# Two-layer S5, Hyena and pooling step: layer 1's scan values computed in the opening, filters and root spread behind the modulation, sums of squares on TensorE, convolutions in turn with gates

## The chip, the core and the metric

One core of a Trainium2 chip runs the whole program. TensorE (PE) multiplies, VectorE (DVE) and ScalarE (ACT) do elementwise work, GpSimd (POOL) does a part of it too, and SyncE (SP) issues most transfers. The metric is the device time of one execution in microseconds (us), lower is better; times are compared as medians of runs.

## The reference

Two layers work on 128 context tokens and 512 latent tokens (T = 640 columns), model width 1024. Cut to what the change touches:

```python
def trunk_layer(x, mod, h0_re, h0_im, p, l):
    shift, scale, gate = jnp.split(mod[:, None, :], 3, axis=-1)      # mod = silu(cond) @ w_mod + b_mod
    h = rms_norm(x, p['norm_g'][l]) * (1.0 + scale) + shift
    proj = h @ p['w_in'][l]
    u_a, g_a, u_b, g_b, u_c, g_c, m = jnp.split(proj, IN_SPLIT_POINTS, axis=-1)
    y_a, st_re, st_im = s5_branch(u_a, ...)       # 32 groups, 64 complex states, two directions
    y_b = hyena_branch(u_b, ...)                  # short convolution, then gated long convolutions
    y_c = pool_branch(u_c, ...)
    ...                                           # silu gates, three branch projections, w_out
    return x + gate * out, st_re, st_im
```

`s5_discretise` turns each state's parameters into a step factor a and an input matrix `bb` = k * b (complex). `hyena_filters` makes a layer's long filters from positions and weights alone; a bias times the input is added to each long convolution. Neither depends on x.

## The kernel before

**Layout.** Channels lie on the partitions, the 640 tokens on the free axis, as two halves of HT = 320 columns or as context (LS = 128 columns) and latents. Every matrix product is a split one: a float32 operand becomes a rounded high part and the rest, and three matmuls are summed: `mm` with (hhi, wh), (hlo, wh), (hhi, wl), lines 261 to 263. A window of 128 output channels is 48 mm of 320 columns. Weights come by SP in pieces `wr`; ACT makes `wh`, DVE `wl` (lines 238, 239). All engines run their instructions in the order in which a scheduler has put them; a DMA stands in its engine's queue, and an instruction behind one that waits has to wait too.

**Opening.** `s5_load`, `setup`, `mlp` (hidden layer of the Hyena filters, for both layers), `load_x0` (x and the position embedding). `square` (line 582) squares each of eight 128-channel blocks on ACT and adds them up on DVE into `acc` (line 589); `rsum` sums over partitions by tiny matmuls `ssq` (line 599). `s5_disc` computes both layers' factors and powers in small DVE operations. `mod_chunk` multiplies the conditioning with w_mod, four chunks of four loads `wm` (line 401) and matmuls `modp`; `mod_turn` transposes the result (`modt`). `s5_disc2` finishes layer 0's scan values: the product `bb` (`cmul`, lines 693 to 698), `phases` (lines 846 to 851), and powers copied by ACT into `pi` and `po`; layer 1's powers and factors go to DRAM (`pwd`, `rsd`). `rinv` makes 1/sqrt of the mean square by three Newton rounds, spreads it over the partitions (`rdg` on DVE, `rbc` on PE, copy `rr` on ACT), and `make_h` forms h for each half: `ht`, `hhi`, `hlo` (lines 656 to 665). `filter` makes a quarter of a layer's Hyena filters: `fw` and `fwp` (line 511) on PE, `hx` and `hq` on DVE, the bias row `br` added by two one-partition DVE operations (lines 522, 523), then `fps` matmuls and a store `hd`.

**A layer.** `u_a` computes four windows and stores them to `ud`; `load_u` reads them back as `ug` in S5 layout. Then eight S5 blocks of four groups: `s5_gen` makes matrices `i`, transposes them on PE (`trp`), forms the local kernel (`khp`), stores it to `kd` and reads it back by eight loads as `mt`, and makes phases `tt`; `s5_run` multiplies (`pz`), scans on DVE, and multiplies back (`yp`). After each block two or three items of a list `beside` run: twelve convolution windows (`conv_u`: ACT copies `raw`, DVE adds the two neighbours in `vx`), then four gates (`gate_b`), then four windows computed ahead (`ahead`). The list goes from front to back:

```python
beside = [lambda i=i: self.conv_u(l, i, vx[i // 4][:, i % 4, :], SP) for i in range(12)]
beside += [lambda i=i: self.gate_b(l, i, S, vx[2]) for i in range(4)]
beside += [lambda i=i: self.ahead(l, 40 + i, AF.Tanh, 0.5, SP) for i in range(4)]
```

**Boundary.** While layer 0's output projection runs, two of layer 1's four filter quarters are made; then `rinv` on POOL, `make_h`, the other two quarters. `s5_prep` loads layer 1's powers and factors and computes there what `s5_disc2` computed for layer 0, with the complex product on POOL.

## Time and profile before

| | |
|---|---|
| median of 3 runs | 1528.35 us (1527.81 to 1533.11) |
| profiled execution, its own time | 1534.17 us |
| its span from first to last instruction | 1532.4 us |
| PE, DVE, ACT, POOL busy | 1435.3, 1125.5, 672.0, 524.9 us |
| mean granted TensorE clock | 0.976 |

Busy time is the sum over the span; the stretches below show where an engine idles. The clock is the share of full speed that the throttle granted.

### The profile page before, as it was taken

How to read it: one execution, taken by the hardware profiler on the slowest of the kernel's cores; microseconds unless marked ns; L12 is line 12 of the kernel's file. 1: busy time of each engine (PE TensorE's matmuls, PEld its weight loads, DVE VectorE, ACT ScalarE, POOL GpSimd, SP SyncE). 2: the span in 40 equal slices, each digit the busy share in tenths (PEclk: the TensorE clock that was granted, in tenths of full speed). 3: DMA queues.
4: the chain of work that ended last, by engine and by line, in shares of the span. 5: the costliest groups of instructions: out<-in, count | busy, mean ns of one | idle time of the engine just before them, and what ended most of it. 6: DMA issues, size and time to landing. Idle time of an engine off the chain costs nothing.

```text
span 1532.4 us, 28365 instructions
## 1 busy us (share of the span) xinstructions
PE 1435.3 (94%) x10812; PEld 1372.2 (90%) x10812; DVE 1125.5 (73%) x1951; ACT 672.0 (44%) x1454; POOL 524.9 (34%) x473
## 2 busy tenths in 40 slices
PE   3998899999999999999998897989999999999997
PEld 1688888999999998999997787989999999999996
DVE  8996998854777795555678879896557778866665
ACT  3574545434333342344345644544443334344443
POOL 0033433500343334553323733443003444166401
PEclk9899999999999999999998899999999999999998
DMA  9535122244322246444752342223622223322154
GB/s 313 188 112 132 57 72 70 71 146 123 99 71 77 76 134 234 157 151 139 230 159 81 110 113 68 71 71 94 172 89 81 83 70 106 115 83 83 35 178 153
DMA packets 120464, 178.74 MB, mean 117 GB/s; under 512 B 33944, under 2 KB 58152, under 8 KB 119817
## 3 DMA queue, kind: packets, MB, share of 16 engines
q1 hardware_dynamic: 115737, 170.58, 36.5%
q0 software_dynamic: 1152, 5.77, 1.1%
q8 instruction: 85, 1.39, 0.4%
q10 hardware_dynamic: 3440, 0.59, 0.2%
q14 instruction: 50, 0.41, 0.1%
HBM read 152.71 MB, written 24.18 MB: 115 GB/s over the span
## 4 chain that ended last, share of the span: by engine, by line
PE 68%; DVE 15%; DMA 6%; issue 5%; ACT 3%; SPq 2%; POOL 1%; POOLq 0%; ACTq 0%; DVEq 0%
PE mm L261 15%; PE mm L263 15%; PE mm L262 15%; PE mm L333 3%; PE mm L335 3%; PE mm L334 3%; DVE wl L239 2%; PE inva L1145 1%; SPq L914 1%; DVE i L874 1%; PE invb L1145 1%; PE yp L976 1%; PE modp L404 1%; DVE vx L1003 1%; DVE hlo L665 1%
## 5 line engine op out<-in xcount | busy, mean ns | idle before, releaser
L261 PE MATMUL mm<-hhi,wh 128*128 128x320 f32 x1408 | 446.1, 318 | 15.3 <-ACT raw L996 9.0
L263 PE MATMUL mm<-hhi,wl 128*128 128x320 f32 x1408 | 440.4, 314 | 8.5 <-DVE wl L239 6.3
L262 PE MATMUL mm<-hlo,wh 128*128 128x320 f32 x1408 | 442.4, 314 | 0.5 <-DVE hlo L659 0.4
L239 DVE TENSOR_TENSOR wl<-wr,wh 128x512 fp32r<-128x512 f32 x316 | 265.9, 843 | 114.4 <-ACT wh L238 111.5
L238 ACT CAST wh<-wr 128x512 fp32r<-128x512 f32 x316 | 195.5, 619 | 269.1 <-PE mm L262 188.9
L261 PEld LDWEIGHTS mm<-hhi,wh 128*128 128x128 f32 x1408 | 269.9, 192 | 20.8 <-ACT raw L996 10.0
L263 PEld LDWEIGHTS mm<-hhi,wl 128*128 128x128 f32 x1408 | 269.5, 192 | 9.5 <-DVE wl L239 6.8
L262 PEld LDWEIGHTS mm<-hlo,wh 128*128 128x128 f32 x1408 | 270.1, 192 | 1.7 <-DVE hlo L659 1.2
L262 PE MATMUL mm<-mlo,wh 128*128 128x320 f32 x256 | 79.6, 312 | 0.5 <-DVE mlo L242 0.4
L261 PE MATMUL mm<-mhi,wh 128*128 128x320 f32 x256 | 79.1, 312 | 0.5 <-ACT wh L238 0.4
L263 PE MATMUL mm<-mhi,wl 128*128 128x320 f32 x256 | 78.8, 309 | 0.4 <-DVE wl L239 0.4
L873 POOL TENSOR_TENSOR ow<-cw,po 128x512 f32<-128x512 f32 x32 | 41.9, 1328 | 96.6 <-PE yp L976 96.5
L875 POOL TENSOR_TENSOR i<-i,i 128x1024 f32<-128x1024 f32 x16 | 40.5, 2529 | 100.6 <-DVE i L873 71.8
L1244 DVE SCALAR_TENSOR_TENSOR mth<-mth,mm 128x320 f32<-128x320 f32 x64 | 31.1, 486 | 52.5 <-PE mm L263 52.5
L1246 POOL TENSOR_TENSOR macc<-macc,mth 128x320 f32<-128x320 f32 x32 | 35.0, 1099 | 86.4 <-DVE mth L1244 86.4
L239 DVE TENSOR_TENSOR wl<-ws,wh 128x512 fp32r<-128x512 f32 x48 | 42.7, 889 | 29.7 <-ACT wh L238 28.6
L333 PE MATMUL mm<-hhi,wh 128*128 128x320 f32 x192 | 59.9, 312 | 0.0
L335 PE MATMUL mm<-hhi,wl 128*128 128x320 f32 x192 | 59.4, 309 | 0.0
L334 PE MATMUL mm<-hlo,wh 128*128 128x320 f32 x192 | 59.4, 309 | 0.0
L238 ACT CAST wh<-ws 128x512 fp32r<-128x512 f32 x48 | 29.8, 621 | 60.2 <-PE mm L334 32.3
L1052 POOL TENSOR_TENSOR ps<-pu 128x663 f32<-128x663 f32 x8 | 12.3, 1540 | 120.4 <-ACT pu L1045 120.4
L1246 POOL TENSOR_TENSOR acc<-acc,mth 128x320 f32<-128x320 f32 x32 | 37.7, 1179 | 44.4 <-DVE mth L1244 44.3
(421 smaller groups left out, 3809.9 us busy)
## 6 DMA issues: line engine op xcount, KB each, us to landing
wr<-w_in SPq DMA_DIRECT2D x224, 256.0 KB, 2.6
wm<-w_mod SPq DMA_DIRECT2D x48, 512.0 KB, 5.4
wr<-w_out SPq DMA_DIRECT2D x48, 256.0 KB, 3.0
hd<-hs SPq DMA_DIRECT2D x32, 256.0 KB, 2.3
hsr<-hd SPq DMA_DIRECT2D x32, 256.0 KB, 2.6
mt<-kd SPq DMA_DIRECT2D x128, 32.0 KB, 1.8
wr<-w_br_a SPq DMA_DIRECT2D x16, 256.0 KB, 2.6
wr<-w_br_b SPq DMA_DIRECT2D x16, 256.0 KB, 2.7
```

The source lines that it names most:

```text
L238: nc.scalar.copy(hi, src)
L239: nc.vector.tensor_tensor(out=lo, in0=src, in1=hi.bitcast(F32), op=ALU.subtract)
L261: nc.tensor.matmul(ps[i], wh[:, ks], at(hi, k, sl), start=(k == 0), stop=False)
L262: nc.tensor.matmul(ps[i], wh[:, ks], at(lo, k, sl), start=False, stop=False)
L263: nc.tensor.matmul(ps[i], wl[:, ks], at(hi, k, sl), start=False, stop=(k == kt - 1))
L333: nc.tensor.matmul(out, wh[:, ks], xh, start=(k == 0), stop=False)
L334: nc.tensor.matmul(out, wh[:, ks], xl, start=False, stop=False)
L335: nc.tensor.matmul(out, wl[:, ks], xh, start=False, stop=(k == 3))
L873: eng.tensor_tensor(out=out[:, r], in0=hb(r), in1=pb(0), op=ALU.mult)
L875: e.tensor_tensor(out=out, in0=out, in1=tmp, op=ALU.add)
L1244: v.scalar_tensor_tensor(out=o[:, sl], in0=th[:, sl], scalar=1.0, in1=ps, op0=ALU.add, op1=ALU.mult)
L1246: nc.gpsimd.tensor_tensor(out=acc[:, sl], in0=acc[:, sl], in1=th[:, sl], op=ALU.add)
```

## The change

1. The opening computes the scan values of both layers (`s5_disc2` loops over the layers). Layer 1's five tiles go by POOL's queue to DRAM (`vd`), and `s5_prep` only loads them. `s5b`, the loaded matrix, and `phq` now share one buffer (tag s5b, one copy). Memsets of `bp` and `bf` move to POOL.
2. In the opening each square is summed directly on PE (`square_pe`); the Newton rounds come before the modulation, the spread (`rspread`) behind its last transpose; filter work on PE also behind that transpose, and w3 and the windows behind the last wm load.
3. At the boundary `rinv` runs on DVE, and `make_h` takes segments of columns (context and latents in the opening).
4. The bias row is added on PE by one more matmul per case, with one row of contraction.
5. `beside` mixes convolutions with ahead windows and gates, two light items to three heavy ones, the last four convolutions first.

```diff
@@ filter
-                                 stop=(i == len(ws) - 1))
+                                 stop=(i == len(ws) - 1 and t not in (2, 4)))
+            if t in (2, 4):
+                r = slice(0, 1) if t == 2 else slice(64, 65)
+                nc.tensor.matmul(fp if t == 4 else fw[:, t], self.k(C_BR)[r], br[r], start=False, stop=True)
...
-        v.tensor_tensor(out=hx[0:1, 2], in0=hx[0:1, 2], in1=br[0:1], op=ALU.add)
-        v.tensor_tensor(out=hq[64:65], in0=hq[64:65], in1=br[64:65], op=ALU.add)
@@ new
+    def square_pe(self, X, kk, half, ps):
...
+        nc.scalar.activation(sq, X[:, kk, half * HT:half * HT + HT], AF.Square)
+        for j in range(nh):
+            c = half * nh + j
+            nc.tensor.matmul(ps[:, c:c + 1], sq[:, j * 64:j * 64 + 64], self.k(C_ONE)[:, 0:1],
...
@@ scan values
-        self.cmul(nc.gpsimd if l else nc.vector, Q, self.bb[:, 0], self.bb[:, 1], kb(kre), kb(kim), sm[:, 0], sm[:, 1], [G, H], "cb")
+        sm = Q.tile([P, 2, G, H], F32, tag="s5b", name="s5b", bufs=1)
         nc.sync.dma_start(sm, self.I['s5m'][l, :, 0:2])
...
+        self.cmul(nc.vector, Q, bb[:, 0], bb[:, 1], kb(kre), kb(kim), sm[:, 0], sm[:, 1], [G, H], "cb")
...
     def s5_disc2(self, Q, S, pw, rs):
         nc = self.nc
-        nc.scalar.dma_start(self.pwd, pw[:, :, :, 1])
-        nc.scalar.dma_start(self.rsd, rs[:, :, 1])
-        self.s5_bb(Q, S, 0, rs[:, 6, 0], rs[:, 7, 0])
-        self.s5_vals(S, 0, pw[:, :, :, 0], rs[:, :, 0])
...
+        for l in range(DEPTH):
+            tl = self.s5_tiles(S if l == 0 else Q)
+            self.s5_vals(Q, l, pw[:, :, :, l], rs[:, :, l], *tl)
+            if l:
+                for d, t in zip(self.vd, tl):
+                    nc.gpsimd.dma_start(d, t)
...
     def s5_prep(self, S):
...
+        tl = self.s5_tiles(S)
+        for d, t in zip(self.vd, tl):
+            self.nc.sync.dma_start(t, d)
+        self.s5_open(S, 1, tl)
@@ opening
-                    dd = self.s5_disc(Q, SP)
+                    ssq = self.PS.tile([P, 512], F32, tag="mm", name="ssq", bufs=3)[0:64, 0:2 * (HT // 64)]
                     for kk in range(KD):
-                        self.square(X, kk, 0)
+                        self.square_pe(X, kk, 0, ssq)
...
+                    y = self.rinv((0, 1), nc.vector, "mm", ps=ssq, spread=False)
+                    self.s5_disc2(Q, SP, *self.s5_disc(Q, SP))
+                    for n in (2, 3, 0, 1):
+                        self.mod_turn(0, n, self.mod_chunk(0, n, M, "mm"), "mm")
+                    with tc.issue_after(self.last_mt.ins):
+                        rr = self.rspread((0, 1), y, "mm")
...
+                    with tc.issue_after(self.last_wm.ins):
+                        self.filter_load(0, F, wins, fr, fh)
...
+                self.make_h(0, X, ((0, LS, 0), (LS, T, 1)), rr)
+                with tc.issue_after(self.last_mt.ins):
+                    for o in range(2):
+                        for hf in range(2):
+                            self.filter(0, o, hf, F)
@@ boundary
-                            rr = [r for r, _ in self.rinv((0, 1), nc.gpsimd, "mm")]
-                            for half in range(2):
-                                self.make_h(l + 1, X, half, rr[half])
+                            rr = self.rinv((0, 1), nc.vector, "mm")
+                            self.make_h(l + 1, X, ((0, HT, 0),), rr)
+                            self.make_h(l + 1, X, ((HT, LS, 0), (LS, T, 1)), rr[:, HT:])
@@ layer
+            heavy = [lambda i=i: self.conv_u(l, i, vx[i // 4][:, i % 4, :], SP) for i in (*range(8, 12), *range(8))]
+            gates = [lambda i=i: self.gate_b(l, i, S, vx[2]) for i in range(4)]
+            ahead = [lambda i=i: self.ahead(l, 40 + i, AF.Tanh, 0.5, SP) for i in range(4)]
+            light = ahead[:2] + gates + ahead[2:]
+            beside = []
+            for i in range(4):
+                h, g = heavy[3 * i:3 * i + 3], light[2 * i:2 * i + 2]
+                beside += [h[0], g[0], h[1], h[2], g[1]]
```

SP's queue in the opening, before (`w_349` is w3, `s5m` holds the S5 matrices, `hyb` the bias rows):

```order
L474 DMA w_349<-hyp 64x1024
L476 DMA wins<-win 128x512 x5
L401 DMA wm<-w_mod 128x1024 x4
L794 DMA s5b<-s5m 128x1024
L811 DMA cw<-s5m 128x1024
L496 DMA br<-hyb 1x256 x4
L252 DMA wr<-w_in 128x512 x3
L401 DMA wm<-w_mod 128x1024 x4
```

The same queue in the changed kernel, from the fifth wm load on (`w_626` is w3):

```order
L403 DMA wm<-w_mod 128x1024 x2
L254 DMA wr<-w_in 128x512 x2
L403 DMA wm<-w_mod 128x1024 x2
L254 DMA wr<-w_in 128x512
L403 DMA wm<-w_mod 128x1024 x3
L815 DMA s5b<-s5m 128x1024
L403 DMA wm<-w_mod 128x1024 x5
L476 DMA w_626<-hyp 64x1024
L478 DMA wins<-win 128x512 x5
```

The filter's loads went from ahead of the first wm to behind the last, and layer 1's `s5b` load now stands ahead of five of the sixteen wm loads.

DVE's queue at the start of layer 1, before, from the second `wl` split of u_a on:

```order
L239 TENSOR_TENSOR wl<-wr,wh 128x512
L846 TENSOR_TENSOR phq<-cst,rsl 128x608
L848 TENSOR_TENSOR ph<-cst,rsl 128x608
L847 TENSOR_SCALAR phq<-phq 128x608
L239 TENSOR_TENSOR wl<-wr,wh 128x512
L849 TENSOR_TENSOR ph<-ph,phq 128x608
L239 TENSOR_TENSOR wl<-wr,wh 128x512
L850 TENSOR_TENSOR phq<-cst,rsl 128x608
L851 TENSOR_TENSOR ph<-ph,phq 128x608
L672 MEMSET ua_9719 128x8
L239 TENSOR_TENSOR wl<-wr,wh 128x512
L873 TENSOR_TENSOR i_9993<-bb,pi 128x512
```

The same place in the changed kernel:

```order
L241 TENSOR_TENSOR wl<-wr,wh 128x512 x2
L943 TENSOR_TENSOR tt<-ph 128x352 x2
L897 TENSOR_TENSOR i_10003<-bb,pi 128x512
L898 TENSOR_TENSOR i_10004<-bb,pi 128x512
L241 TENSOR_TENSOR wl<-wr,wh 128x512
```

The six phase operations are gone, and the first block's `tt` and `i` stand right behind the first splits.

ACT's queue in layer 0's fourth S5 block, before (`z` copies take the starting states, `kh` is the local kernel):

```order
L906 COPY kh<-khp 128x240
L892 COPY bf_453<-bb 128x8x16
L238 CAST wh<-wr 128x512
L956 COPY z<-rsl 64x8
L957 COPY z<-rsl 64x8
L996 COPY raw<-mm 128x320
L925 ACTIVATE d_2676<-cst,rsl 128x82 x4
```

The block in the changed kernel that answers to it:

```order
L930 COPY kh<-khp 128x240
L916 COPY bf_504<-bb 128x8x16
L1006 ACTIVATE gu<-gu 128x324
L240 CAST wh<-wr 128x512
L1020 COPY raw<-mm 128x320
L980 COPY z<-rsl 64x8
L981 COPY z<-rsl 64x8
```

The convolution's first `raw` copy moved from behind the z copies to ahead of them here; in four of layer 0's eight blocks it stands behind them in the changed kernel.

## Rows read from the trace of the kernel before

**Rows 1.** The page's busy times: us, share of the span, instructions.

```profile
PE 1435.3 (94%) x10812; PEld 1372.2 (90%) x10812; DVE 1125.5 (73%) x1951; ACT 672.0 (44%) x1454; POOL 524.9 (34%) x473
```

**Rows 2.** Table of stretches: length, busy us (instructions), PEclk, DMA share, GB/s.

```profile
0.00:60.00 60.00, 32.17 (x154) 15.95 (x155) 51.87 (x174) 25.82 (x55) 1.47 (x6) 0.91 0.93 305
100.00:345.00 245.00, 224.43 (x2025) 218.11 (x2024) 197.69 (x263) 116.13 (x293) 92.28 (x61) 0.97 0.34 95
345.00:800.00 455.00, 453.85 (x3178) 434.79 (x3176) 297.90 (x538) 178.17 (x344) 158.06 (x161) 1.00 0.43 137
800.00:900.00 100.00, 83.99 (x589) 78.01 (x590) 78.88 (x132) 57.69 (x131) 45.88 (x43) 0.90 0.39 112
900.00:1050.00 150.00, 134.10 (x1295) 130.14 (x1294) 135.44 (x186) 75.14 (x195) 66.48 (x40) 0.97 0.24 69
1100.00:1500.00 400.00, 397.47 (x2769) 392.96 (x2770) 283.17 (x497) 167.17 (x325) 144.12 (x141) 1.00 0.32 96
```

**Rows 3.** PE's waits, whole span: waiting line, releaser, us, times, longest.

```profile
PE yp L974 <- DMA mt<-kd: 19.5, 9, 3.7
...
PE mm L261 <- ACT raw L996: 9.0, 4, 3.1
PE mm L263 <- DVE wl L239: 6.7, 3, 5.0
PE pz L944 <- DMA ug<-ud: 5.0, 2, 3.3
PE modp L404 <- DMA wm<-w_mod: 4.3, 1, 4.3
```

**Rows 4.** PE's timeline at the boundary: start, duration, line, tile; idle before.

```profile
799.08 0.28 PE L599 MATMUL ssq<-cst,acc 128*64 128x1 f32 x2
...
808.24 0.39 PE L599 MATMUL ssq<-cst,sq 128*64 128x1 f32 x4
...
820.09 1.85 PE L635 MATMUL rbc<-rdg,cst 64*128 64x320 f32 x4
...
824.96 0.31 PE L261 MATMUL mm<-hhi,wh 128*128 128x320 f32 x1
...
894.85 0.28 PE L944 MATMUL pz<-ug,it 128*64 128x82 f32 x1 [1.69 <-DMA ug<-ud]
```

**Rows 5.** The mm alone, by stretches: PE, PEld, DVE, ACT busy, PEclk.

```profile
71.20:145.00 73.80, 44.92 (x286) 42.09 (x286) 0.00 (x0) 7.15 (x16) 1.00 0.42 112
824.90:894.80 69.90, 51.77 (x292) 48.13 (x292) 0.00 (x0) 7.10 (x16) 0.90 0.43 120
```

**Rows 6.** Prices: timeline rows; the last is fps alone in a stretch.

```profile
854.73 1.65 DVE L850 TENSOR_TENSOR phq<-cst,rsl 128x608 f32<-128x608 f32 x1
...
855.69 1.85 POOL L697 TENSOR_TENSOR bb<-cb,cb 128x512 f32<-128x512 f32 x1
...
44.09 0.69 DVE L695 TENSOR_TENSOR cb<-rs,s5b 128x512 f32<-128x512 f32 x1
...
22.68 0.48 DVE L589 TENSOR_TENSOR acc<-acc,sq 128x320 f32<-128x320 f32 x1
...
39.61 1.99 PE L511 MATMUL fw<-w,fh 64*128 64x256 f32 x8
...
71.20:145.00 73.80, 15.13 (x115) 14.07 (x114) 6.58 (x12) 1.00 0.42 112
```

**Rows 7.** DMA: a POOL-queue load's row, and the tile wm's issues and landings.

```profile
fr<-fdft POOLq DMA_DIRECT2D x2, 1152.0 KB, 6.3
...
L401 SPq DMA_DIRECT2D wm<-w_mod x16: 327/328/384, 15.2 to 51.5; - x16
...
DMA to landing us min/median/max: 4.1/4.7/5.4
```

**Rows 8.** ACT's timeline in layer 0's fourth S5 block.

```profile
197.59 0.20 ACT L956 COPY z<-rsl 64x8 f32<-64x8 f32 x1 [6.89 <-DVE z L955]
```

**Rows 9.** Layer 0: first `ht` on DVE, first `pz` on PE.

```profile
71.23 0.53 DVE L661 SCALAR_TENSOR_TENSOR ht<-X,sg,rr 128x320 f32<-128x320 f32 x1
...
144.99 0.28 PE L944 MATMUL pz<-ug,it 128*64 128x82 f32 x1 [3.32 <-DMA ug<-ud]
```

More of the change, by code (lines that the diff above doesn't have):

```diff
@@ L116, in constants @@
     cst[:, CO[C_MAG]] = MAGIC
+    for r in (0, 64):
+        cst[r, CO[C_BR] + r] = 1.0 / (1.0 + f32(0.05))
     fmax = 15
@@ L608, in newton, with rinv @@
         e.tensor_tensor(out=y, in0=y, in1=t, op=ALU.mult)
-    def rinv(self, halves, e, tag="b", root=False):
+    def rinv(self, halves, e, tag="b", root=False, ps=None, spread=True):
         nc = self.nc
@@ L613, in rinv @@
         n = nh * len(halves)
-        ps = self.rsum(halves, tag)
+        if ps is None:
+            ps = self.rsum(halves, tag)
         x = self.N.tile([64, n], F32, tag="rx", name="rx", bufs=2)
@@ L643, in new_h, with make_h @@
         self.hlo = self.HP.tile([P, KD, T], F32R, tag="hlo", name="hlo")
-    def make_h(self, l, X, half, rr):
+    def make_h(self, l, X, segs, rr):
         nc = self.nc
         sm, sg = self.smod[l]
-        t0 = half * HT
+        base = segs[0][0]
         for kk in range(KD):
-            t = self.N.tile([P, HT], F32, tag="ht", name="ht", bufs=2)
-            for s, e, _, ci in self.segs(half):
+            t = self.N.tile([P, segs[-1][1] - base], F32, tag="ht", name="ht", bufs=2)
+            for s, e, ci in segs:
@@ L668, in u_a @@
+                nc.scalar.activation(hi, tv, AF.Identity, bias=b)
+                nc.vector.scalar_tensor_tensor(out=lo, in0=tv, scalar=b, in1=hi.bitcast(F32),
+                                               op0=ALU.add, op1=ALU.subtract)
     def u_a(self, l, S, uas):
@@ new lines, in s5_disc2, with s5_vals @@
+        self.s5_open(S, 0, keep)
+    def s5_vals(self, Q, l, pw, rs, bb, ph, pi, po, rsl):
+        nc = self.nc
+        self.s5_bb(Q, bb, l, rs[:, 6], rs[:, 7])
+        gv = lambda a: a.rearrange("p t g -> p g t")
+        for r, ri, ro in ((0, 0, 0), (1, 2, 1)):
+            nc.scalar.copy(pi[0:64, ri], gv(pw[0:64, r, 0:8, :])[:, :, ::-1])
+            nc.scalar.copy(pi[64:P, ri], gv(pw[64:P, r, 0:8, :]))
+            nc.scalar.copy(po[0:64, ro], gv(pw[0:64, r, 1:9, :]))
+            nc.scalar.copy(po[64:P, ro], gv(pw[64:P, r, 1:9, :])[:, :, ::-1])
+        nc.scalar.mul(pi[:, 1], pi[:, 2], -1.0)
+        nc.scalar.mul(po[:, 2], po[:, 1], -1.0)
+        nc.scalar.copy(rsl, rs[:, 0:6])
+        v = nc.vector
+        sh = [P, G, NA + NBW]
+        mb = self.k(C_MT).unsqueeze(1).to_broadcast(sh)
+        fb = lambda i: rs[:, 1 + i].unsqueeze(2).to_broadcast(sh)
+        q = Q.tile([P, 2, G, H], F32, tag="s5b", name="phq", bufs=1).rearrange("p r g h -> p (r g h)")
+        q = q[:, 0:G * (NA + NBW)].rearrange("p (g m) -> p g m", g=G)
+        v.tensor_tensor(out=q, in0=mb, in1=fb(0), op=ALU.mult)
+        v.tensor_scalar(q, q, MAGIC, MAGIC, op0=ALU.add, op1=ALU.subtract)
+        v.tensor_tensor(out=ph, in0=mb, in1=fb(1), op=ALU.mult)
+        v.tensor_tensor(out=ph, in0=ph, in1=q, op=ALU.subtract)
+        v.tensor_tensor(out=q, in0=mb, in1=fb(2), op=ALU.mult)
+        v.tensor_tensor(out=ph, in0=ph, in1=q, op=ALU.add)
@@ L1406, in layer @@
             self.load_u(l, S)
-            beside = [lambda i=i: self.conv_u(l, i, vx[i // 4][:, i % 4, :], SP) for i in range(12)]
-            beside += [lambda i=i: self.gate_b(l, i, S, vx[2]) for i in range(4)]
-            beside += [lambda i=i: self.ahead(l, 40 + i, AF.Tanh, 0.5, SP) for i in range(4)]
+            heavy = [lambda i=i: self.conv_u(l, i, vx[i // 4][:, i % 4, :], SP) for i in (*range(8, 12), *range(8))]
[6 more added lines that the diff above has]
+                beside += [h[0], g[0], h[1], h[2], g[1]]
             for b in range(NB):
```

127 lines of the change are left out of this document (47 added, 80 removed).

## The prediction

> **What bounds the kernel now.** I read the page's busy times first. TensorE (PE) is busy for 94% of the span of 1532.4 us [rows 1], so some 97 us of idle PE are all that can be won, and what a change is worth depends on where that idle time lies. The table of stretches shows it [rows 2]. Three stretches matter: 0 to 60 us, PE busy 32.17 of 60; 100 to 345 us (the end of layer 0's u_a and its S5 blocks), idle 20.6; and 800 to 1050 us (the boundary to layer 1, then its S5 blocks), idle 16.0 + 15.9. The granted clock is 0.97, 0.90 and 0.97 in the last three of these. From 345 to 800 and from 1100 to 1500 us PE is full (453.85 of 455, 397.47 of 400) at clock 1.00; no edit takes PE work from there, and I carry them over unchanged. In the S5 stretch from 900 us DVE is as full as PE (135.44 of 150).
>
> The list of PE's waits [rows 3] says who ends the idle time: the S5 blocks' `mt` loads 19.5 us in 9 waits, the `raw` copies of the convolutions 9.0 in 4, `wl` 6.7 in 3, `wm` 4.3 in one.
>
> Last I followed the boundary in PE's timeline [rows 4]. The sums of the root start at 799.08, their last group at 808.24, the spread of the root (`rbc`) only at 820.09, the first mm of u_a at 824.96, the first S5 block's `pz` at 894.85: 95.8 us in all. What an mm costs is read from the stretches of mm alone [rows 5]: 286 in 44.92 us at clock 1.00 before layer 0's pz, 0.157 each, but 292 in 51.77 us at 0.90 before layer 1's.
>
> **Layer-1 boundary.** *Ceiling.* From 800 to 900 us PE idles 16.0 us, and a clock of 0.90 over 100 us is 10 us of lost work: 26 us. *Removed.* Six phase operations on DVE (the longest kinds 1.65 [rows 6]), six products on POOL (up to 1.85 [rows 6], while the same product took 0.69 on DVE in the opening [rows 6]) and eleven ACT copies. In the trace they ran around 855 us [rows 6] beside u_a, with the `wl` splits queued among them on DVE, and the S5 transposes behind them. *Moved.* The root's Newton steps go from POOL to DVE, a few us earlier; all filter operations now stand ahead of rbc or before the boundary, and 192 mm of u_a stand in one run behind. *Added.* Five loads of the stored values, 1.72 MB, where two small loads stood. They wait for make_h's last read of X, whose memory they take. The nearest row is POOL's `fr`, 1152 KB landing in 6.3 us [rows 7]: the S5 preparation can wait 0 to 6 us for them; I take 2, since u_a runs meanwhile and the first that is needed is the smallest case (DVE's `tt`).
>
> The chain after, on PE, from the first root sum: root, spread and first mm at about 22 instead of 25.9. Then 286 mm (45), small S5 matmuls (2), gaps as in layer 0 (2 to 5): pz at 71 to 74, against 95.8, so 22 to 25 us. PE work that moved ahead of the boundary comes off: 30 filter matmuls at 0.13 (115 in 15.13 us [rows 6]) and four bias matmuls at 0.5 (below), 6 us. Less the 2 us for the loads, **15 us** gained. Bounds: 6 (the loads cost 6 and the root gets no earlier) and 20 (the loads cost nothing).
>
> **S5 blocks of both layers.** Convolutions and gates now take turns; a gate or ahead window needs no pass on DVE over 642 columns, so the early blocks, which held three and two convolutions, ask less of DVE. At 197.59 us two `z` copies on ACT ran after 6.89 us of waiting for DVE [rows 8], and a raw copy that PE needed stood right behind them. In that block the raw copy now stands ahead of the z copies, but in four of layer 0's eight blocks it still stands behind; there it is DVE's shorter queue that must help. So of the 9.0 us of raw waits I expect two thirds to go, 6 us, and with them a part of the work lost to low clock: 0.97 over 245 and 150 us is 12 us, of which I take 2. The mt waits stay in the sum: their chain (kernel matmuls, copy, store to `kd`, eight loads) is unchanged. **8 us** for two layers. Bounds: 0 (gate waits take the raw waits' place) and 22 (all of raw, half of mt and a third of the clock's loss).
>
> **Opening.** DVE loses 14 `acc` additions of 0.48 [rows 6], 6.7 us, and gains layer 1's product and phases, twelve operations of about 0.7, 8.4 us. ACT gains eleven copies. The squares' sums are 80 tiny matmuls, 40 more, where PE idles: nothing; if that cover is gone, some 3 us. The memsets and stores that POOL takes over hold up nothing on POOL itself, which has no other work there. The filters' DVE work that ran ahead of make_h moves behind it.
>
> There the change has a hitch. Layer 1's matrix load `s5b` shares one buffer with layer 0's, so it waits until DVE is through with layer 0's phases, which I put at 45 us from DVE's rows; five of the 16 `wm` loads stand behind it on SP's queue. The last wm was issued at 51.5 us, and they land in 4.1 to 5.4 us [rows 7]; I now put the last landing at 55 to 61, and the last modulation transposes at 58 to 64, so the first `ht` comes at 60 to 67 instead of 71.23 [rows 9]. But all of the filters' PE work now stands behind the modulation, where a good part of it ran between the wm loads before. From there to pz: 16 `fw` and four `fwp` at 0.5 (four took 1.99 us [rows 6]), 10 us; 168 filter matmuls, 22; 292 mm, 46; small ones 3; eight bias matmuls.
>
> A bias matmul has one row of contraction and 256 f32 columns. None like it is in the trace; the nearest row is the opening's f32 fw, 0.5 us, and I take that; between 0.13 (the filters' f32r ones) and 0.5 it is 1 to 4 us for layer 0. Sum 85 us, with 3 for gaps: pz at 146 to 152 against 144.99 [rows 9]. **4 us** lost, bounds −5 (the bias matmuls and gaps cheap, wm early) and +12.
>
> On such a matmul the Trainium skill ("TensorE: Matmul & The Clock Gate") says that a matmul's time goes by its columns and not by its contraction rows. By that the bias matmul costs as much as fw, which is the value taken; no row here shows it.
>
> **Sum.** 4 − 15 − 8 = −19 us. Against the profiled execution's 1534.2 that is 1515; it was 5.8 us over the median of the three runs, 1528.35. Taken off the median: **1509**. A measurement of this kernel tells about 0.5%, 7.6 us, from no change.
>
> **Rivals.** *A: the turn in the S5 blocks brings nothing* (0.22). DVE is what the blocks wait for; the raw waits become gate waits and mt stays. For it: 19.5 us of mt against 9.0 of raw, DVE at 90%. Against: a raw copy stood idle behind a DVE wait. Time 1528 − 15 + 4 = 1517. *B: everything comes in* (0.18). The opening gains 5, the boundary 20, S5 18: 1485. It needs the s5b wait to end by 40 us. *C: no change* (0.1). The boundary gives 8 because the loads or DVE hold it, S5 nothing, the opening takes 4: 1524. *D: slower* (0.1). One mechanism, the queue behind `s5b` on SP. ACT has 16 copies of layer values ahead of the copy that empties the third modulation chunk, and if DVE's phases end at 65 us instead of 45, wm lands 20 us later, the first ht comes at 82 to 87, and pz at 168 to 174. With 23 us of gain left, the change turns slower when layer 0's pz comes after 168; at 35 us of loss in the opening the time is 1540.
>
> A rule that bears on D: by the Trainium skill ("SBUF — State Buffer", on DVE and DMA issued by GpSimd) GpSimd writes such a transfer's descriptors over a port that DVE can hold, and it advises the queue of ACT or SP. The stores of layer 1's values move to GpSimd's queue while DVE is at its fullest (51.87 of 60 [rows 2]). No row here has such a store beside a busy DVE: `fr` went out at the start. If it holds, memory that the new h takes over comes free late, as in D, without any late wm.
>
> **Numbers.** The forecast's own case has 0.4 (1501 to 1516). The range that leaves out about 0.2 goes from B's end to a little past C's: **1484 to 1528**. Faster by over 0.5% (under 1520.7): 0.4 + 0.18 (B) + 0.16 of A's 0.22, 0.74. Within 0.5%: C and the rest of A, 0.16. Slower: 0.10.
>
> **What would show it.** Boundary: the first mm 22 us after the first root sum, no scan-value operations on DVE or POOL there, pz at 71 to 75. S5: raw waits of 3 us in all at most, mt still 15 to 20, the clock 0.98 or more. Opening: first ht at 60 to 67, layer 0's pz at 146 to 152, a wm wait in PE's list. I am wrong if layer 0's pz comes after 160, if waits for gates or `tt` replace the raw waits, or if layer 1's pz waits over 6 us for the five loads.

## The result: slower, and the profile after

The changed kernel took 1541.88 us (median of 4, 1540.41 to 1544.38) against 1528.08 for the kernel before, measured beside it; the ratio is 1.0085 (1.0059 to 1.0111). That is slower by more than the 0.5% bound, and outside the range 1484 to 1528. The two profiled executions lie 6.2 us apart (span 1532.4 and 1538.6), since that of before was high among its runs (1534.17) and that of after its lowest (1540.41): the traces below account for 6.2 of the 13.8 us, the rest shows in medians only. Of all executions behind the ratios of this document one is left out, of the kernel e18 below: it took 6443.72 us. (The section on the kernel calls LS the context's 128 columns; LS is the 512 latents.)

First the page of the kernel after, busy times over the span:

```profile
PE 1460.0 (95%) x10964; PEld 1383.4 (90%) x10964; DVE 1089.2 (71%) x1920; ACT 671.9 (44%) x1445; POOL 516.5 (34%) x465
```

Against [rows 1] PE is busy 24.7 us longer, with 152 records more, while the span grew by 6.2: PE's idle time fell by 18.5 us, and more than that came back as work. To see where, both spans are cut at the same landmarks (first `pz` of layer 0, its last `trp`, first root sum, first `pz` of layer 1, its last `trp`). The kernel before, then the kernel after; columns: stretch, length, busy of PE, PEld, DVE, ACT, POOL, granted clock, DMA share, GB/s:

```profile
0.00:145.00 145.00, 108.23 (x700) 85.71 (x700) 121.36 (x301) 75.19 (x168) 29.75 (x28) 0.94 0.61 189
145.00:321.70 176.70, 163.37 (x1499) 158.61 (x1500) 152.74 (x205) 84.14 (x215) 69.33 (x42) 0.95 0.26 75
321.70:799.10 477.40, 476.25 (x3400) 457.05 (x3398) 309.58 (x555) 185.43 (x362) 159.37 (x166) 1.00 0.44 138
799.10:894.90 95.80, 79.79 (x541) 73.75 (x540) 76.62 (x128) 55.92 (x128) 45.88 (x43) 0.89 0.39 114
894.90:1070.00 175.10, 159.21 (x1493) 155.02 (x1494) 150.93 (x205) 84.04 (x215) 70.10 (x42) 0.97 0.26 74
```

```profile
0.00:163.20 163.20, 133.89 (x841) 104.43 (x842) 110.02 (x264) 78.14 (x165) 29.98 (x32) 0.86 0.57 181
163.20:337.00 173.80, 158.57 (x1493) 153.65 (x1494) 141.60 (x213) 84.17 (x216) 74.45 (x45) 0.98 0.27 79
337.00:822.30 485.30, 483.52 (x3437) 462.03 (x3435) 314.46 (x559) 189.87 (x371) 158.81 (x166) 1.00 0.43 137
822.30:907.30 85.00, 78.76 (x513) 69.50 (x512) 63.92 (x119) 47.96 (x113) 32.99 (x28) 0.88 0.46 128
907.30:1075.30 168.00, 156.11 (x1499) 151.57 (x1499) 141.99 (x204) 82.62 (x211) 71.12 (x42) 1.00 0.28 80
```

Row by row: the opening is 18.2 us longer, 25.7 more busy and 7.5 less idle. Layer 0's S5 blocks gain 2.9, layer 1's 7.1. The full stretch between loses 7.9, all of it busy time: `fps` went from 42 records (5.82 us) to 72 (10.21 us), moved ahead of the boundary, and four bias matmuls are new there (2.78 us). The boundary gains 10.8, nearly all idle (16.0 to 6.2). The stretch after layer 1's S5 loses 0.9. One caution on the clock column: over the first 29 us of both kernels it reads 1.00, though a `modp` record takes 1007 and 1059 ns on average between 18 and 29 us and 598 ns at full speed in the kernel before (66 to 78 us). So the 0.94 and 0.86 of the opening are too high.

What PE did in the opening of the kernel after, grouped by line to 163 us (busy, mean ns of one, idle before):

```profile
L406 PE MATMUL modp<-wm,cs 128*32 128x512 f32 x64 | 19.0, 935 | 1.9 <-DMA wm<-w_mod 1.8
L602 PE MATMUL ssq<-cst,sq 128*64 128x1 f32 x160 | 15.8, 231 | 13.1 <-ACT sq L599 13.1
L513 PE MATMUL fw<-w,fh 64*128 64x256 f32 x32 | 10.7, 463 | 0.0
L417 PE MATMUL modt<-cst,mp 128*128 128x2 f32 x32 | 5.8, 304 | 1.5 <-ACT mp L409 1.5
L517 PE MATMUL fwp<-br,cst 1*128 1x256 f32 x8 | 3.3, 497 | 0.0
L517 PE MATMUL fw<-br,cst 1*128 1x256 f32 x8 | 3.3, 496 | 0.0
```

The same view of the kernel before:

```profile
L404 PE MATMUL modp<-wm,cs 128*32 128x512 f32 x64 | 15.2, 810 | 4.3 <-DMA wm<-w_mod 4.3
L511 PE MATMUL fw<-w,fh 64*128 64x256 f32 x32 | 7.9, 386 | 0.6 <-DVE hx L520 0.6
L415 PE MATMUL modt<-cst,mp 128*128 128x2 f32 x32 | 4.2, 254 | 0.8 <-ACT mp L407 0.7
L599 PE MATMUL ssq<-cst,sq 128*64 128x1 f32 x20 | 1.9, 221 | 0.0
L599 PE MATMUL ssq<-cst,acc 128*64 128x1 f32 x20 | 1.6, 202 | 0.0
```

The one-column sums went from 3.5 to 15.8 us, the bias matmuls are 6.6 new, and unchanged work (`modp`, `fw`, `modt`) became dearer by 3.8, 2.8 and 1.6. The last is the clock. Windows of the kernel after (columns as above):

```profile
40.00:60.00 20.00, 12.35 (x72) 6.79 (x68) 10.51 (x23) 12.66 (x28) 1.62 (x3) 0.50 0.66 213
60.00:80.00 20.00, 18.51 (x56) 9.72 (x57) 11.74 (x32) 6.80 (x14) 3.49 (x3) 0.59 0.55 199
```

0.50 is the lower level, 1.2 GHz; before had 0.91 and 0.83 in these windows. The first `ht` came at 72.1 us, against 71.23 before. Why `h` starts no earlier is read in the queue of PE (start, duration, what it waited for) and, below, in that of ACT at the same time:

```profile
39.16 3.16 PE L406 MATMUL modp<-wm,cs 128*32 128x512 f32 x8 [1.79 <-DMA wm<-w_mod]
49.83 2.29 PE L602 MATMUL ssq<-cst,sq 128*64 128x1 f32 x20 [7.52 <-ACT sq L599]
52.06 1.86 PE L417 MATMUL modt<-cst,mp 128*128 128x2 f32 x8
...
62.45 6.09 PE L406 MATMUL modp<-wm,cs 128*32 128x512 f32 x16
69.29 1.05 PE L417 MATMUL modt<-cst,mp 128*128 128x2 f32 x8 [0.74 <-ACT mp L409]
```

```profile
36.69 0.64 ACT L844 COPY pi<-pw 64x256 f32<-64x256 f32 x1 [1.99 <-DVE pw L718]
...
46.42 0.62 ACT L847 COPY po<-pw 64x256 f32<-64x256 f32 x1
...
49.33 0.45 ACT L599 ACTIVATE sq<-X 128x320 f32<-128x320 f32 x1
...
51.28 0.56 ACT L409 COPY mp<-modp 128x512 f32<-128x512 f32 x1
```

ACT makes the copies of both layers, 16 of 0.62 to 0.65 us, and the small ones behind them from 36.7 to 49.3. Two things that PE needs stand behind them: one of the last squares, and the copy `mp` of the second modulation chunk. That chunk's `modp` ended at 42.32; its `mp` began 9 us later, at 51.28, and ended at 51.84, and the transposes that read it started at 52.06. PE's wait of 7.52 us bears the name of the square, because the sums of that square stand ahead of the transposes in PE's queue. But without the sums the transposes could not have started before 51.84 either: what holds them up is ACT's copies. The next `wm` loads wait in turn, up to 10.7 us, for `modp` to free a buffer. The last transposes end at 70.3.

The waits of PE after, in all, to compare with [rows 3] (total, times, longest):

```profile
PE ssq L602 <- ACT sq L599: 13.1, 2, 7.5
PE yp L998 <- DMA mt<-kd: 12.7, 8, 2.8
PE mlpp L463 <- DMA w<-hyw: 9.8, 1, 9.8
PE yp L1000 <- DVE w L992: 9.3, 9, 1.8
PE mm L263 <- ACT raw L1020: 6.6, 5, 2.3
```

Last the boundary of the kernel after, in PE's timeline, beside [rows 4]:

```profile
822.31 0.74 PE L613 MATMUL ssq<-cst,acc 128*64 128x1 f32 x10
...
843.61 0.80 PE L656 MATMUL rbc<-rdg,cst 64*128 64x320 f32 x2
...
848.24 0.31 PE L263 MATMUL mm<-hhi,wh 128*128 128x320 f32 x1
...
907.25 0.40 PE L968 MATMUL pz<-ug,it 128*64 128x82 f32 x1
```

The root takes as long as before (first mm 25.9 us after the first sum in both). Its Newton rounds, on DVE now, run from 827.13 to 841.18 between other operations; on POOL before they ran from 809.23 to 814.95. From the first mm to `pz` it is 59.0 instead of 69.9.

### The profile page after: what moved, and what is told of

It is laid out like the page before. It is cut to its first block, busy times and chain, and to the rows that moved or that the text cites. A ratio compares the mean times of both kernels' runs of the same rounds, so it can differ in the third digit from the quotient of the medians.

```text
span 1538.6 us, 28658 instructions
## 1 busy us (share of the span) xinstructions
PE 1460.0 (95%) x10964; PEld 1383.4 (90%) x10964; DVE 1089.2 (71%) x1920; ACT 671.9 (44%) x1445; POOL 516.5 (34%) x465
## 4 chain that ended last, share of the span: by engine, by line
PE 69%; DVE 15%; DMA 5%; issue 5%; ACT 3%; POOL 2%; SPq 1%; POOLq 0%; DVEq 0%; ACTq 0%
PE mm L265 14%; PE mm L263 14%; PE mm L264 14%; PE mm L335 3%; PE mm L337 3%; PE mm L336 3%; DVE wl L241 2%; PE modp L406 2%; DVE i L898 2%; PE inva L1169 1%; PE invb L1169 1%; PE yp L1000 1%; DVE kk L986 1%; DVE kk L985 1%; DVE i L897 1%
## 5 line engine op out<-in xcount | busy, mean ns | idle before, releaser
L264 PE MATMUL mm<-mlo,wh 128*128 128x320 f32 x256 | 79.6, 312 | 0.5 <-DVE mlo L244 0.4
L899 POOL TENSOR_TENSOR i<-i,i 128x1024 f32<-128x1024 f32 x16 | 45.6, 2850 | 56.8 <-DVE i L897 55.5
```

The lines of the kernel that those rows point to most:

```text
L264: nc.tensor.matmul(ps[i], wh[:, ks], at(lo, k, sl), start=False, stop=False)
L899: e.tensor_tensor(out=out, in0=out, in1=tmp, op=ALU.add)
```

## The experiments

The question: which part of the opening costs the 18 us. My theory was the queue: the late modulation (rival D's place), by the `s5b` wait and ACT's copies. Its rivals: PE's added work (one-column sums, bias matmuls) at low clock; the filter work held behind the modulation, which then stands on the path; `make_h` by segments; the values themselves. Beside that: the turn of convolutions and gates alone, and the Newton rounds on DVE alone. All ratios are to the kernel before, measured beside each; times are of one profiled execution of each kernel. Executions of one kernel lie up to 15 us apart (e1: 1527.21 to 1542.24), so a landmark that moves by 2 or 3 us shows little. The changed kernel itself was measured only once, beside a before of 1528.08; the before of the others lay at 1529.61 to 1531.18, so 0.1 to 0.2% of each share that is called "back" below may be the reference's. "Transposes" is the end of the last `modt`.

| kernel | ratio (95%) | transposes | layer 0 pz | root sum | layer 1 pz | span |
|---|---|---|---|---|---|---|
| before | 1 | 77.0 | 145.0 | 799.1 | 894.9 | 1532.4 |
| after | 1.0085 (1.0059, 1.0111) | 70.3 | 163.2 | 822.3 | 907.3 | 1538.6 |
| e1_s5b_early | 1.0030 (1.0008, 1.0051) | 67.7 | 163.5 | 819.6 | 899.2 | 1531.9 |
| e9_copies_pool | 1.0038 (1.0016, 1.0060) | 64.6 | 160.4 | 817.6 | 899.4 | 1535.5 |
| e4_squares_first | 1.0041 (1.0019, 1.0063) | 67.9 | 161.9 | 819.8 | 901.5 | 1537.9 |
| e6_bias_dve | 1.0040 (1.0023, 1.0058) | 71.3 | 164.7 | 809.9 | 896.7 | 1534.6 |
| e5_squares_dve | 1.0077 (1.0052, 1.0101) | 69.9 | 164.8 | 822.6 | 907.1 | 1542.0 |
| e3_no_hold | 1.0073 (1.0052, 1.0095) | 82.9 | 166.2 | 822.0 | 902.1 | 1539.9 |
| e7_values_back | 1.0113 (1.0091, 1.0134) | 66.1 | 158.9 | 818.1 | 910.3 | 1545.5 |
| e8_three_together | 1.0085 (1.0061, 1.0110) | 77.2 | 170.0 | 817.1 | 905.8 | 1539.3 |
| e12_pool_early_bias | 0.9988 (0.9965, 1.0011) | 65.0 | 156.5 | 803.7 | 889.8 | 1525.3 |
| e10_no_hold_values_back | 1.0083 (1.0054, 1.0112) | 77.0 | 159.4 | 813.9 | 908.2 | 1542.7 |
| e13_and_squares_back | 1.0059 (1.0036, 1.0082) | 72.9 | 155.2 | 805.9 | 898.0 | 1532.9 |
| e14_and_bias_back | 1.0132 (1.0112, 1.0152) | 75.1 | 159.1 | 809.3 | 911.0 | 1548.6 |
| e15_values_pool_only | 0.9978 (0.9965, 0.9991) | 81.8 | 156.2 | 800.8 | 888.6 | 1523.1 |
| e17_pool_early_bias_nohold | 1.0006 (0.9992, 1.0020) | 77.9 | 157.3 | 806.9 | 893.3 | 1530.0 |
| e19_halves_again | 1.0034 (1.0013, 1.0055) | 83.0 | 162.1 | 816.2 | 905.6 | 1536.4 |
| e18_segments_only | 0.9998 (0.9975, 1.0021) | 80.4 | 150.4 | 801.4 | 899.0 | 1535.7 |
| e2_turn_only | 0.9949 (0.9934, 0.9964) | 76.3 | 143.6 | 790.7 | 885.9 | 1516.0 |
| e11_turn_rinv_dve | 0.9944 (0.9925, 0.9963) | 78.6 | 145.7 | 792.1 | 889.4 | 1523.0 |

### The queue in the opening

**e1_s5b_early**, the phases' scratch laid into `bb`, so that `s5b` waits for layer 0's products alone:

```diff
-        self.s5_bb(Q, bb, l, rs[:, 6], rs[:, 7])
...
-        q = Q.tile([P, 2, G, H], F32, tag="s5b", name="phq", bufs=1).rearrange("p r g h -> p (r g h)")
+        q = bb.rearrange("p r g h -> p (r g h)")
...
         v.tensor_tensor(out=ph, in0=ph, in1=q, op=ALU.add)
+        self.s5_bb(Q, bb, l, rs[:, 6], rs[:, 7])
```

> The changed kernel, but the phases' scratch lies in bb instead of in the buffer of the loaded matrix, so layer 1's s5b load waits only for layer 0's products (about 36 us instead of 44), and twelve wm loads instead of eleven stand ahead of it. Theory S (the SP queue behind s5b makes the opening late): the first ht comes 6 to 8 us earlier than 72.1, layer 0's first pz at about 156, the time falls by about 7 us to 1535. Theory F (filter work that stands whole behind the modulation makes it late): first ht a little earlier, pz stays within 3 us of 163, time within 3 us of 1541.9. The scheduler also puts the squares ahead of the layer copies on ACT here, so a gain speaks for S or for theory A (below), not for F.

Ratio 1.0030: 0.55% of after's time back. The copies on ACT now stand ahead of the copy `mp` (45.7 to 59.8), and `modt` waits 7.4 us for it: the wait changed its name, and layer 0's pz did not move (163.5). Its gain lies at the root sum (2.7) and the boundary (79.6 us instead of 84.9).

**e9_copies_pool**, the 16 copies and the negations on POOL:

```diff
-            nc.scalar.copy(pi[0:64, ri], gv(pw[0:64, r, 0:8, :])[:, :, ::-1])
+            nc.gpsimd.tensor_copy(pi[0:64, ri], gv(pw[0:64, r, 0:8, :])[:, :, ::-1])
...
-        nc.scalar.mul(pi[:, 1], pi[:, 2], -1.0)
+        nc.gpsimd.tensor_scalar(pi[:, 1], pi[:, 2], -1.0, None, op0=ALU.mult)
```

> The changed kernel with the 20 copies and negations of pi and po of both layers on POOL, which has nothing to do there, instead of on ACT. Theory A (in every variant so far these 10 to 14 us of ACT copies stand ahead of the copy that empties a modulation chunk, or of a square, and PE waits 5 to 7 us for it): no ACT wait of PE over 2 us between 30 and 70 us, the last modulation transposes end by 63 instead of 70, layer 0's first pz at 154 to 157, time 6 to 8 us below the changed kernel's, ratio 1.003 to 1.005. Theory H (the whole filter work behind the modulation sets pz, whatever ends first ahead of it): pz stays at 160 to 164, ratio 1.006 or more.

**e4_squares_first**, the copies only after the last square:

```diff
+        with self.tc.issue_after(self.last_sq.ins):
+            for r, ri, ro in ((0, 0, 0), (1, 2, 1)):
```

> The changed kernel with ACT's copies of pi and po ordered behind its last square. Theory A (ACT's copies ahead of the squares, and PE's sums of squares ahead of modp and modt, stop PE for 7.5 us at half clock after): the ssq wait of 7.5 us goes, the first ht comes 7 us earlier, the time falls by 7 to 12 us to 1530 to 1535. Theory S or F: the copies only move ahead of the copy that empties a modulation chunk, first ht and time within 3 us of the changed kernel's.

0.47% and 0.44% back (by the medians alone 4.6 and 3.8 us). In e4 PE waits 5.0 us for `mp` instead of 7.52 for the square. In e9 the transposes end 5.8 us earlier, but pz comes only 2.8 earlier. The stretch before and after the last transposes in e9 says why (columns as above):

```profile
0.00:64.60 64.60, 42.48 (x265) 25.17 (x265) 52.20 (x166) 19.24 (x43) 25.94 (x35) 0.82 0.83 280
64.60:160.30 95.70, 92.79 (x576) 81.96 (x576) 62.88 (x98) 47.85 (x102) 23.93 (x17) 0.89 0.38 119
```

Behind the transposes PE is full, 92.8 of 95.7 us, and the clock there is lower than in after. The same cut in after and in before:

```profile
0.00:70.30 70.30, 43.93 (x265) 25.14 (x265) 47.19 (x166) 30.42 (x63) 5.60 (x15) 0.78 0.83 282
70.30:163.20 92.90, 89.97 (x578) 79.29 (x578) 62.83 (x98) 47.72 (x102) 24.37 (x17) 0.93 0.36 104
```

```profile
0.00:77.00 77.00, 49.17 (x257) 29.81 (x258) 66.79 (x212) 34.42 (x72) 2.73 (x7) 0.89 0.76 251
77.00:145.00 68.00, 59.07 (x445) 55.90 (x444) 54.58 (x90) 40.76 (x97) 27.02 (x21) 1.00 0.44 118
```

So the last transposes are not late against before: they end 6.7 us *earlier*. What is longer is the rest, 92.9 instead of 68.0, with 30.9 us more PE work in it. Ahead of the transposes before does 49.2 us of work with some 3 of sums in it; after does 43.9, of which 15.8 are sums. So some 18 us of other work went from ahead of the transposes to behind them; the bias matmuls bring 6.6, and the mm to pz, partly at low clock, keep PE busy for 49.3 us (292 of them) instead of 44.9 (286).

The kernels that keep the hold and have all 16 copies on ACT (after, e1, e4, e5, e6, e8) agree on the front: from 36 us on PE waits once for 5.0 to 7.5 us for an ACT instruction behind the copies, a square or `mp`, and the last transposes end at 67.7 to 77.2. With the copies on POOL (e9, e12) the longest wait for ACT is 2.7 and 0.7 us, and they end at 64.6 and 65.0; with layer 0's eight copies alone (e7) it is 3.9 us, and they end at 66.1.

### The added work and the holds

**e5_squares_dve** puts the squares' additions back on DVE, as before (`acc`, 20 records of sums):

```diff
-                        self.square_pe(X, kk, 0, ssq)
+                        self.square_acc(X, kk, 0, acc)
```

> The changed kernel with the sums of squares taken back from TensorE: DVE adds the squares in place (14 additions), and 10 tiny matmuls instead of 80 stand in PE's queue. Theory P (the 80 f32 matmuls, two passes each, stand in PE's queue ahead of the modulation, wait for ACT there, and hold PE up at half clock): the 15.8 us of ssq and its 13.1 us of waits go, the last modulation transposes end 8 to 12 us earlier than 70, layer 0's first pz at 150 to 154, the time falls by 8 to 12 us, to 0.3% over before or less. Theory V (layer 1's values on DVE and ACT set the opening, the squares only lie beside them): pz stays at 160 to 163, ratio 1.006 to 1.009.

Nothing (1.0077). The sums fall from 15.8 to 2.0 us, but the work is taken where PE idles for another reason, ahead of the transposes (30.49 us busy of 69.9); these end at 69.9, and 94.9 us follow. The other reason is the copies on ACT, and the second chunk's transposes now wait for `mp` by name:

```profile
51.70 1.86 PE L417 MATMUL modt<-cst,mp 128*128 128x2 f32 x8 [6.56 <-ACT mp L409]
```

**e6_bias_dve** puts the bias row back on DVE:

```diff
-            if t in (2, 4):
-                r = slice(0, 1) if t == 2 else slice(64, 65)
-                nc.tensor.matmul(fp if t == 4 else fw[:, t], self.k(C_BR)[r], br[r], start=False, stop=True)
...
+        v.tensor_tensor(out=hx[0:1, 2], in0=hx[0:1, 2], in1=br[0:1], op=ALU.add)
+        v.tensor_tensor(out=hq[64:65], in0=hq[64:65], in1=br[64:65], op=ALU.add)
```

> The changed kernel with the bias row of the filters added on DVE again (16 operations of 0.41 us) instead of by 16 one-row matmuls. By the trace of the changed kernel these matmuls take 6.6 us of PE before layer 0's first pz (half of it at half clock) and about 5 at the boundary. If they are on the path: pz 4 to 6 us earlier, 8 us in all, ratio about 1.004. If PE waits there anyway: within 2 us of the changed kernel.

0.45% back, though not in the opening: pz 164.7, but the root sum comes 12.4 us earlier, from shorter S5 blocks and 7.5 us less in the full stretch.

**e3_no_hold** leaves out the two kinds of hold (filters and spread behind the last `modt`, loads behind the last `wm`):

```diff
-                    with tc.issue_after(self.last_mt.ins):
-                        rr = self.rspread((0, 1), y, "mm")
+                    rr = self.rspread((0, 1), y, "mm")
...
-                with tc.issue_after(self.last_mt.ins):
-                    for o in range(2):
+                for o in range(2):
```

> The changed kernel without the three holds: root spread, filters and filter loads of layer 0 go wherever the scheduler puts them. Theory F: filter work runs in the modulation's idle time again, layer 0's first pz returns to 145 to 150, the time falls by 12 to 18 us to 1524 to 1530. Theory A (layer 1's values and squares in ACT's and PE's queues make it late): first ht stays at 72 or later, pz at 158 or later, time within 5 us of 1541.9.

```profile
0.00:82.90 82.90, 61.95 (x335) 36.88 (x335) 55.34 (x180) 35.24 (x72) 5.61 (x15) 0.84 0.76 253
82.90:166.20 83.30, 78.23 (x505) 71.83 (x505) 59.29 (x93) 44.81 (x98) 27.52 (x20) 0.88 0.38 106
```

Without the holds 18 us more work runs ahead of the transposes, but the transposes come 12.6 us later; pz stays at 166. So taking the holds out alone brings nothing; PE has 140 us of work before pz in e3 (before: 108).

**e7_values_back** computes layer 1's values at the boundary again, as before:

```diff
-        for l in range(DEPTH):
-            tl = self.s5_tiles(S if l == 0 else Q)
-            self.s5_vals(Q, l, pw[:, :, :, l], rs[:, :, l], *tl)
...
+        nc.scalar.dma_start(self.pwd, pw[:, :, :, 1])
+        nc.scalar.dma_start(self.rsd, rs[:, :, 1])
```

> The changed kernel with layer 1's scan values made at the boundary again, as before the change. Theory V: the opening gets 8 us or more earlier (first ht at 62 to 64 instead of 72.1), the boundary loses 8 to 12, the time stays within 4 us. Theory P: the opening gains 3 us at most, the boundary loses 8 to 12, the time rises to 1548 or more, ratio 1.012 or more.

1.0113, an interval that overlaps that of after: the opening gains 4.3, the boundary loses 7.3 (92.2 from root sum to pz instead of 84.9). By these landmarks moving the values is a net gain of some 3 us, which is not clear of noise; the cause of the loss it is not.

### Together

**e8_three_together** is e1, e5 and e6 in one kernel; **e12_pool_early_bias** is e1, e6 and e9; **e17_pool_early_bias_nohold** is e12 with e3's edit; **e15_values_pool_only** is e17 with e5's. Three cuts of e12's edit:

```diff
         for r, ri, ro in ((0, 0, 0), (1, 2, 1)):
-            nc.scalar.copy(pi[0:64, ri], gv(pw[0:64, r, 0:8, :])[:, :, ::-1])
+            nc.gpsimd.tensor_copy(pi[0:64, ri], gv(pw[0:64, r, 0:8, :])[:, :, ::-1])
...
-            if t in (2, 4):
...
-        q = Q.tile([P, 2, G, H], F32, tag="s5b", name="phq", bufs=1).rearrange("p r g h -> p (r g h)")
+        q = bb.rearrange("p r g h -> p (r g h)")
```

> Early s5b load, squares on DVE and bias on DVE together, all else as in the changed kernel. If the three losses add: 8 + 10 + 6 us off the changed kernel, ratio 0.992 to 0.995, layer 0's first pz at 146 to 150. If they cover one another (one queue behind the other): ratio 1.000 to 1.003, pz at 152 or later.

> The changed kernel with the copies on POOL, the early s5b load and the bias row on DVE. If the three add (6, 3 and 6 us of the opening, 3 at the boundary): layer 0's first pz at 150 or earlier, ratio 0.997 to 1.000. If theory H holds, pz at 155 or later and the ratio 1.002 or more.

> As the third run, with the squares' sums on TensorE. If the tiny matmuls are what costs: pz 7 to 10 us later than in the third run, ratio 0.997 to 1.000. If not: within 3 us of it.

> No holds, squares and bias row on DVE, but layer 1's values made in the opening with the copies on POOL and the early s5b load. If the values cost the opening little then (DVE 8 us, ACT nothing): pz at 150 to 153, boundary 84 to 86 us from root to pz, ratio 0.990 to 0.994, better than the turn alone. If DVE sets the opening: pz at 156 or later, ratio 0.996 or more.

e8 brings nothing (1.0085; transposes at 77.2, and again 92.7 us behind them). e12 wins back the whole loss: 0.9988, the same as before. In its profile layer 0's pz is 6.7 us earlier than in after, the root sum 18.7. e15 is at 0.9978, e17 at 1.0006. None of the three brings pz back to 145. e15 and e17 differ in the sums alone: PE is busy for 113.1 and 131.7 us before pz, and pz comes at 156.2 and 157.2.

**e10_no_hold_values_back** is e3 and e7; **e13_and_squares_back** adds e5; **e14_and_bias_back** adds e6 to that, so that of the change little is left but `make_h`'s segments, the place of the Newton rounds and loads, the boundary's order and the turn.

```diff
-                    with tc.issue_after(self.last_wm.ins):
-                        self.filter_load(0, F, wins, fr, fh)
+                    self.filter_load(0, F, wins, fr, fh)
...
-            self.s5_vals(Q, l, pw[:, :, :, l], rs[:, :, l], *tl)
+        self.s5_vals(S, 0, pw[:, :, :, 0], rs[:, :, 0])
```

> The changed kernel without the three holds and with layer 1's values made at the boundary: what is left of the change in the opening is the squares' sums and the bias row on TensorE. Theory H: with the values out of ACT's and DVE's way the filters fill the modulation's idle time as before the change; pz at 148 to 152, the boundary as in the run with the values back (92 us from the root to pz), time about 1533, ratio 1.000 to 1.004. If the tiny matmuls and the bias row are what makes the opening late: pz at 158 or later, ratio 1.008 or more.

> No holds, values at the boundary, squares' sums on DVE again; the bias row still on TensorE. If the 120 passes of tiny matmuls fill PE: pz from 159.4 to 150 to 153, ratio about 1.003. If the bias row does: pz stays at 156 or later, ratio 1.007 or more.

> As the run before it, and the bias row on DVE again. What is left of the change is the turn, the root on DVE and make_h by context and latents. pz at 144 to 148 as in the kernel before, boundary as in the turn with the root on DVE, ratio 0.993 to 0.997. If make_h's order by segments costs something: pz at 150 or later.

1.0083, 1.0059, 1.0132: undone part by part, the change does not lead back to before. e14 has as little work in the opening as e18 (116.4 us busy to pz; 115.9), but pz at 159.1; PE waits 11.4 us for `raw` and 11.0 for `wl`, more than before in both. That these times hang on the order that the scheduler makes from the whole program, and not on the edits alone, is my reading and not shown. One difference stays in all seven kernels without the hold: they load the windows `wins` at 18 to 24 us and run the first `fps` at 55.7 to 69.1, while before, e2, e11 and e18 load them at 11.6 to 15.2 and run the first `fps` at 49.4 to 56.6. No kernel put the place of these loads, and the order of the code around them, back by itself; this rival is untested.

**e18_segments_only** is before with layer 0's `make_h` by latents and context; **e19_halves_again** is e15 with it by halves again.

```diff
-                for half in range(2):
-                    self.make_h(0, X, half, rr[half])
+                self.make_h(0, X, ((0, LS, 0), (LS, T, 1)), rr)
```

> The kernel before with layer 0's make_h over latents and context together, nothing else in the opening. Theory M (u_a's first window needs all eight blocks of one half; with both halves in one pass it gets them when DVE and ACT are through with all of h): first ht unchanged within 2 us of 71.2, PE idles more between 80 and 120, pz at 150 to 154, ratio 1.003 to 1.006. Rival (the order of the code around the modulation makes e14 late, not make_h): pz within 2 us of 145, ratio within 0.002 of 1.

> The run with values on POOL, no holds, squares and bias row on DVE, and layer 0's make_h half after half again. Theory M: pz 4 to 8 us earlier than 156.2, ratio 0.992 to 0.995. Rival: pz and time as in that run within 2 us, ratio 0.996 to 0.999.

0.9998 and 1.0034: segments cost no time in before, and halves in e15 make it slower, so by the ratios the theory fell. Its landmark did come in e18 (pz at 150.4, forecast 150 to 154), but in one execution of 1537.48 us, 7 over its median.

### The turn and the root alone

**e2_turn_only** is before with the new list alone:

```diff
-            beside = [lambda i=i: self.conv_u(l, i, vx[i // 4][:, i % 4, :], SP) for i in range(12)]
...
+            light = ahead[:2] + gates + ahead[2:]
+            for i in range(4):
+                h, g = heavy[3 * i:3 * i + 3], light[2 * i:2 * i + 2]
+                beside += [h[0], g[0], h[1], h[2], g[1]]
```

> The kernel before with the new turn of convolutions, gates and ahead windows alone. My account of the traces gives the turn 3 us in layer 0 and 7 in layer 1: 1518 us, 0.993 of before. Rival: these gains come from the shorter work ahead of the blocks (other DVE and DMA work), then it is within 2 us of 1528.

0.9949, 7.8 us faster by the ratio. **e11_turn_rinv_dve** is e2 with the boundary's Newton rounds on DVE:

```diff
-                            rr = [r for r, _ in self.rinv((0, 1), nc.gpsimd, "mm")]
+                            rr = [r for r, _ in self.rinv((0, 1), nc.vector, "mm")]
```

> The kernel before with the new turn and with the boundary's Newton steps on DVE, nothing else. If the boundary's gain is in the root: the spread comes 4 to 5 us earlier than the 21 us after the first root sum, 3 us less than the run with the turn alone, ratio 0.992 to 0.994. If DVE's queue takes it back: as the turn alone, 0.995.

0.9944, the same as e2 within the intervals; `rbc` comes 25.3 us after the root sum, against 21.1 in e2. These two are the best versions of the study, ahead of both kernels.

## Why the prediction was wrong

**Opening: the step that failed.** The text said "last modulation transposes at 58 to 64", then 85 us of PE work "with 3 for gaps", pz "at 146 to 152", "**4 us** lost". Measured: transposes 70.3, then 92.9 with PE busy for 89.97, pz 163.2, 18.2 lost. So the transposes were 6 to 12 us later than forecast and the work behind them was 5 us more. The `s5b` wait itself came as reckoned (45 us; the load was issued at 44.24), and PE waited only 1.8 us for `wm`. Four terms were wrong:
- ACT's "eleven copies" more had no price in the sum. The 16 copies, with what stood behind them, put 9 us between the second chunk's `modp` and its `mp`. I had named them in rival D, for the third chunk. With them on POOL the transposes end at 64.6 (e9), near the forecast.
- The 80 tiny matmuls "where PE idles: nothing; if that cover is gone, some 3 us". They are 160 records and 15.8 us, and 60 more than before, not "40 more" (before had 20, in 40 records). They did not make the opening late: e5 took them to 2.0 us, and transposes and pz stayed at 69.9 and 164.8.
- The bias matmuls: 6.6 us for layer 0, not 4. Each is two overlapping records of 0.50, 0.82 together. By the Trainium skill ("TensorE: Matmul & The Clock Gate", Step-by-step: what each phase is for) a matmul goes by the columns that stream through, so one row costs as much as many. The trace agrees: 497 ns a record for one row, 463 for `fw`'s 64, over both clock levels.
- The clock: the price list was that of full speed, while PE ran at 0.50 to 0.59 from 40 to 80 us. `fw` and `fwp` took 10.7 and 3.1 us instead of 10 together, mm 49.3 instead of 46. What share of the 18 us this is was not tried by itself.

What the experiments show is narrower than a single cause. In all nine kernels that keep the hold (after, e1, e4 to e9, e12) the last transposes end between 64.6 and 77.2, and pz follows 91.6 to 95.8 us later, with PE busy for 85.2 to 92.9 of these: there pz is the end of the transposes plus the work that the hold leaves behind them. That work is 30.9 us more in after than in before, bias matmuls and lower clock included, while the transposes came only 6.7 earlier. In those without the hold the transposes end between 72.9 and 83.0 and pz follows 74 to 84 us later. PE's added work before pz is not the cause by itself: e15 and e19 have 113.1 and 115.2 us of it, near the 108.2 of before, and pz at 156.2 and 162.1. e12, with copies, `s5b` and bias row changed together, takes back the whole loss in time, and 6.7 of the 18.2 us in pz. Which order of instructions would bring back pz at 145 with the values in the opening stays open.

**Boundary: half right.** "First mm 22 us after the first root sum" is wrong: 25.9, as before. The Newton rounds ended 18.9 us after that sum on DVE, against 15.9 on POOL before, and in e11, where they alone moved, `rbc` came 4.2 us later than in e2: the move that should have won "a few us" won none. "No scan-value operations there, pz at 71 to 75": 84.9. From first mm to pz 10.9 us were won, by less waiting (11.9 to 5.6 us idle there) and less work (58.0 to 53.5; 44 `fps` records ran there before, 2 after); but the clock stayed at 0.88, where I had counted on mm at full speed (286 took 51.9 us, not 45), and the work moved ahead costs 7.9 in the full stretch (6 reckoned). The net is 3, not 15. The five loads made nobody on PE wait.

**S5 blocks: right in size, not in mechanism.** 10.0 us by the traces for 8 predicted, 7.8 by e2's ratio. But `raw` fell only from 9.0 to 6.6 (forecast 3 at most), `mt`, forecast unchanged, from 19.5 to 12.7, and a wait of 9.3 us for DVE's `w` in `yp` came instead (0.6 before). Most of the gain, 7.9 us, is busy time, at a clock of 0.98 and 1.00 instead of 0.95 and 0.97.

**Rivals.** D came true in sign: the change is slower, and the copies on ACT that it names held up an `mp`, though not by way of `wm` or of late phases. Its point did not hold: I had put it at a layer 0 pz after 168, with 23 us of gain elsewhere; at 163 it was slower already, since the boundary gave 3 and not 15. The sign "I am wrong if layer 0's pz comes after 160" applied. For the port that DVE can hold, the Trainium skill ("SBUF — State Buffer", Who interferes with whom) warns of late descriptors of GpSimd's transfers: here five stores were issued at 27 to 62 us, and no wait of PE for them shows. Nothing speaks for it in this kernel.
